# Expert gates scattered into device memory instead of spread by one-hot products

## The chip, the cores and the metric

One core of a Trainium2 chip runs the whole program. TensorE (PE) multiplies, VectorE (DVE) and ScalarE (ACT) work element by element, GpSimd (POOL) does small arithmetic and issues some DMAs, SyncE (SP) issues the DMAs that stream the weights. The metric is the device time of one execution in microseconds (us): the median of three runs of the kernel before is 2316.43 us (2314.47 to 2318.4).

## The reference, cut to what matters

The program is one transformer block (attention and pooling side by side, then a convolutional feed-forward part) and then two layers, each an attention part and a mixture of 16384 single-neuron experts ("peer"), for 256 tokens of width 1024 in float32. The change is in the expert part:

```
q = (x @ w_q).reshape(t, 8, 2, 128)                  # 8 heads, two halves
sc = einsum('thpc,hpnc->thpn', q, sub_keys)          # 128 keys in each half
v_half, i_half = top_k(sc, 16)
cand = v_half[:,:,0,:,None] + v_half[:,:,1,None,:]
cand_idx = i_half[:,:,0,:,None] * 128 + i_half[:,:,1,None,:]
top_s, pos = top_k(cand.reshape(t, 8, -1), 16)
expert = take_along_axis(cand_idx, pos)              # 8 x 16 experts per token
g = softmax(top_s)
act = gelu(einsum('thkd,td->thk', u_tab[expert], x))
y = einsum('thk,thkd->td', g * act, v_tab[expert])
```

Two heads may choose the same expert for a token; their gates then add up.

## The kernel before, in words

The kernel computes all 16384 experts for all tokens and multiplies by a gate that is zero wherever an expert was not chosen. Expert (i, j) has i = 0 to 127 on the partitions and j = 0 to 127 in the loops, and A is a resident tile of 128 x 128 x 256 (i, j, token). Each of the two `peer` layers has three stages.

In `route` 16 tiles of `w_q` give the queries and the scores, and `top16` picks 16 of 128 on DVE. What follows from the scores (candidate sums s0, candidate ids s1, second top-16 s2, the lookup of the chosen ids s4, softmax s3, s3e and s5, transposes s6) is put as small pieces into a list, `self.bg`. In `u_phase` the first expert product runs over 128 values of j: `self.st.get()` fetches a weight tile, `ws_part` issues 24 matmuls into a `tmp` tile, `pop_bg(1)` takes one piece from the list, and every second j `gelu` evicts two columns of A. In `peer` itself the second product follows: `split` turns two columns of A into a rounded part `whi` (ACT) and a remainder `wlo` (DVE), and `acc_k` multiplies them with the tiles of `v`.

The weights come through `Stream`: SP loads a tile of 512 KB into one of four `raw` buffers, ACT rounds it into `hi` (line 86), DVE takes the remainder `lo` (line 87; in `route` POOL does so for every second tile), and three such pairs can be ready ahead of the matmuls. Each engine works in program order, so a `lo` waits behind whatever piece was put on DVE before it.

The gates get into A by one-hot products. When the list is empty, `u_phase` takes four tokens per j: `build` (lines 1372 to 1375) makes on DVE one-hot rows for i and j and multiplies the rows for j by the gate in two float16 parts, and `spread` (lines 1382 and 1383) multiplies them on PE, 8 matmuls for four tokens, so that a bank holds the four tokens' gates for all (i, j). Columns of A that are not computed yet receive the gates by ACT (line 1387); those that are get multiplied by DVE (line 1389). 64 such groups per layer cover 256 tokens. The one-hot rows lie in `xo`, the tile that also holds the residual x, so x is written to device memory (`keep`) at the start of `peer` and read back behind `u_phase`.

Around it: `ffn` is the feed-forward part of the first block. While it runs, `side_step` prepares a vector for its end (`mod`, line 657), to which DVE adds a row `sl` that POOL loads at the start of `ffn`. `gx` and `sl` are constant tiles of 128 x 1024 that several stages use in turn.

Of the kernel before, what the change touches and what calls it, by code (L numbers as in the profile page):

```python
# [20 lines left out]
P = 128  # L21
# [23 lines left out]
class Stream:  # L45
# [56 lines left out]
    def get(self, ahead=NPART):  # L102
        while len(self.ready) < ahead and self.next_item < len(self.items):
            self._prepare()
        return self.ready.popleft()

# [125 lines left out]
class Body:  # L232
# [1002 lines left out]
    def route(self, rt, cv, sk, hi, lo):  # L1235
# [31 lines left out]
        slots = self.sl.bitcast(F16).rearrange("p (i t w) -> p i t w", i=4, w=2)  # L1267
        IT, JT, WH, WL = (slots[:, i] for i in range(4))
        self.slots = (IT, JT, WH, WL)
# [7 lines left out]

        for t in range(2):
# [8 lines left out]
            st["si"] = cv.tile([P, 128], I32, name=f"si{t}")  # L1287
            st["iji"] = cv.tile([P, 2, 128], I32, name=f"iji{t}")
            st["ij"] = cv.tile([P, 2, 128], F32, name=f"ij{t}")
# [8 lines left out]
            bg.append(s0)  # L1298
            bg.append(s1)
            for h in range(0, 8, 2):  # L1300
# [4 lines left out]
                bg.append(s2)  # L1305
# [9 lines left out]
            for h in range(8):  # L1315
                bg.append(lambda h=h, st=st: s4(h, st))

# [7 lines left out]
            bg.insert(len(bg) - 6, s3)  # L1325
            bg.insert(len(bg) - 3, s3e)

            def s5(st=st):
# [4 lines left out]
                nc.vector.tensor_scalar(den, den, WSHIFT, None, op0=OP.mult)  # L1333
                nc.vector.tensor_tensor(e, e, den[:, :, None].to_broadcast([P, 8, 16]), op=OP.mult)
                nc.vector.tensor_copy(st["si"], st["sid"].rearrange("p h k -> p (h k)"))
                nc.vector.tensor_single_scalar(st["iji"][:, 0, :], st["si"], 7, op=OP.arith_shift_right)
# [14 lines left out]
            bg.extend([lambda: None] * 2)  # L1351
            bg.append(s6)

    def u_phase(self, rt, A, hi, lo):

# [274 lines left out]
```

## Time and profile before

| what | us |
|---|---|
| median of 3 runs | 2316.43 (2314.47 to 2318.4) |
| the profiled execution, whole | 2315.69 |
| its span, first to last instruction | 2313.9 |
| PE busy | 2198.4 (95%) |
| DVE busy | 1655.4 (72%) |
| ACT busy | 1098.5 (47%) |
| POOL busy | 160.9 (7%) |
| first layer: `route` about 533 to 588, `u_phase` 588 to 989, second product 989 to about 1330 | |
| second layer: `u_phase` from about 1550, second product to the end | |

An engine's busy time counts overlapping instructions once. [...] The granted TensorE clock is 0.984 of full speed over the span.

### The profile page before, as it was taken

What the parts mean: (1) busy time and instruction counts of PE and PEld (TensorE: products, weight loads), DVE (VectorE), ACT (ScalarE), POOL (GpSimd) and SP (SyncE); (2) the same over time, 40 slices, a digit from 0 to 9 for tenths busy, and PEclk for the clock granted to TensorE, in tenths of its full rate; (3) what the DMA queues carried; (4) which work ended last, traced back from release to release, by engine and by line L of the source; (5) the groups of instructions that cost most, each with busy time, mean ns of one, the idle gap of its engine ahead of it and who ended that gap; (6) DMA issues with size and microseconds to landing.
All of it is one profiled execution on the core that took longest, in us unless ns stands there. A gap on an engine that the chain in (4) does not pass through costs nothing.

```text
span 2313.9 us, 37763 instructions
## 1 busy us (share of the span) xinstructions
PE 2198.4 (95%) x14526; PEld 1988.2 (86%) x14526; DVE 1655.4 (72%) x3410; ACT 1098.5 (47%) x1726; POOL 160.9 (7%) x237
## 2 busy tenths in 40 slices
PE   4888998999999999999999988899999999999998
PEld 3668987778999999988888877799999999888886
DVE  6777755868998899555555565689989985555555
ACT  3445544454444444444444444444444444444444
POOL 2520001303000000000000012120000000000000
PEclk9998999999999999999999999999999999999999
DMA  8856554425565444656666653355544565666664
GB/s 276 317 184 192 177 181 139 141 91 169 175 182 167 156 156 156 210 186 195 192 193 195 189 164 94 114 169 183 183 156 156 156 191 182 191 193 195 193 192 136
DMA packets 114069, 408.88 MB, mean 177 GB/s; under 512 B 12784, under 2 KB 14288, under 8 KB 113632
## 3 DMA queue, kind: packets, MB, share of 16 engines
q1 hardware_dynamic: 110064, 392.71, 53.7%
q0 software_dynamic: 3824, 13.76, 1.9%
q8 instruction: 114, 1.87, 0.3%
q14 instruction: 67, 0.55, 0.1%
HBM read 402.75 MB, written 3.15 MB: 175 GB/s over the span
## 4 chain that ended last, share of the span: by engine, by line
PE 85%; DVE 6%; POOL 2%; ACT 2%; issue 2%; DMA 2%; SPq 0%; POOLq 0%; ACTq 0%; DVEq 0%
PE tmp L483 13%; PE tmp L484 13%; PE tmp L485 13%; PE acc L496 11%; PE acc L497 11%; PE acc L499 11%; DVE lo L87 1%; PE acc L1382 1%; PE acc L1383 1%; PE acc L445 1%; PE acc L446 1%; PE acc L444 1%; POOL rp L526 1%; PE acc L483 1%; PE acc L484 1%
## 5 line engine op out<-in xcount | busy, mean ns | idle before, releaser
L87 DVE TENSOR_TENSOR lo<-raw,hi 128x1024 fp32r<-128x1024 f32 (+3 forms) x683 | 829.8, 1216 | 464.9 <-ACT hi L86 464.0
L86 ACT ACTIVATE hi<-raw 128x1024 fp32r<-128x1024 f32 (+2 forms) x702 | 733.9, 1047 | 554.7 <-PE acc L499 387.3
L483 PE MATMUL tmp<-hThi,hi 128*128 128x256 f32 x2456 | 708.1, 288 | 0.0
L484 PE MATMUL tmp<-hTlo,hi 128*128 128x256 f32 x2456 | 694.0, 283 | 0.0
L485 PE MATMUL tmp<-hThi,lo 128*128 128x256 f32 x2456 | 693.7, 282 | 0.0
L484 PEld LDWEIGHTS tmp<-hTlo,hi 128*128 128x128 f32 x2456 | 470.3, 191 | 0.2 <-issue 0.2
L483 PEld LDWEIGHTS tmp<-hThi,hi 128*128 128x128 f32 x2456 | 470.0, 191 | 0.2 <-ACT hi L86 0.2
L485 PEld LDWEIGHTS tmp<-hThi,lo 128*128 128x128 f32 x2456 | 469.8, 191 | 0.0
L496 PE MATMUL acc<-hi,whi 128*128 128x512 f32 x1024 | 398.6, 389 | 2.4 <-ACT whi L1210 2.4
L497 PE MATMUL acc<-lo,whi 128*128 128x512 f32 x1024 | 398.4, 389 | 0.0
L499 PE MATMUL acc<-hi,wlo 128*128 128x512 f32 x1024 | 315.3, 389 | 0.0
L496 PEld LDWEIGHTS acc<-hi,whi 128*128 128x128 f32 x1024 | 192.2, 188 | 42.6 <-ACT whi L1210 2.8
L497 PEld LDWEIGHTS acc<-lo,whi 128*128 128x128 f32 x1024 | 192.3, 188 | 39.9
L499 PEld LDWEIGHTS acc<-hi,wlo 128*128 128x128 f32 x1024 | 192.2, 188 | 39.9
L1398 ACT ACTIVATE A<-tmp 128x512 f32<-128x512 f32 (+31 forms) x106 | 50.2, 473 | 176.7 <-PE tmp L485 176.7
L1387 ACT ACTIVATE A<-acc 128x328 f32<-128x328 f32 (+31 forms) x128 | 44.9, 351 | 127.9 <-PE acc L1383 127.9
L445 PE MATMUL acc<-lo,hThi 128*128 128x512 f32 (+2 forms) x224 | 88.5, 395 | 10.3 <-DVE lo L87 8.5
L444 PE MATMUL acc<-hi,hThi 128*128 128x512 f32 (+2 forms) x224 | 93.7, 418 | 4.1 <-ACT hi L86 2.0
L446 PE MATMUL acc<-hi,hTlo 128*128 128x512 f32 (+2 forms) x224 | 88.1, 393 | 1.4 <-DVE hTlo L331 1.1
L1211 DVE TENSOR_TENSOR wlo<-A,whi 128x512 fp32r<-128x512 f32 x128 | 87.3, 684 | 0.0
L1210 ACT ACTIVATE whi<-A 128x512 fp32r<-128x512 f32 x128 | 78.3, 613 | 0.0
L1403 DVE TENSOR_TENSOR A<-gx,A 128x512 f32<-128x512 f32 (+16 forms) x84 | 41.6, 496 | 45.6 <-ACT gx L1401 45.5
(394 smaller groups left out, 2730.8 us busy)
## 6 DMA issues: line engine op xcount, KB each, us to landing
raw<-in_uT SPq DMA_DIRECT2D x256, 512.0 KB, 3.5
raw<-in_v SPq DMA_DIRECT2D x256, 512.0 KB, 4.3
raw<-in_w_up SPq DMA_DIRECT2D x44, 512.0 KB, 4.0
adaraw<-in_wada SPq DMA_DIRECT2D x32, 512.0 KB, 5.4
raw<-in_w_q SPq DMA_DIRECT2D x32, 512.0 KB, 3.6
raw<-in_w_down SPq DMA_DIRECT2D x22, 512.0 KB, 3.6
raw<-in_w_in SPq DMA_DIRECT2D x20, 512.0 KB, 5.2
raw<-in_hyb_w_in SPq DMA_DIRECT2D x20, 512.0 KB, 3.7
```

Source lines behind the costliest of these rows:

```text
L86: nc.scalar.activation(hi[:, :width], t[:, :width], AF.Copy)
L87: eng.tensor_tensor(lo[:, :width], t[:, :width], hi[:, :width].bitcast(F32), op=OP.subtract)
L444: nc.tensor.matmul(ps[t][:, :w], xh, wh, start=s, stop=False)
L445: nc.tensor.matmul(ps[t][:, :w], xh, wl, start=False, stop=False)
L446: nc.tensor.matmul(ps[t][:, :w], xl, wh, start=False, stop=e)
L483: nc.tensor.matmul(ps[:, sl], wh, hi[:, k, sl], start=k == 0, stop=False)
L484: nc.tensor.matmul(ps[:, sl], wh, lo[:, k, sl], start=False, stop=False)
L485: nc.tensor.matmul(ps[:, sl], wl, hi[:, k, sl], start=False, stop=k == 7)
L496: nc.tensor.matmul(ps[t][n], h, wh, start=first, stop=False)
L497: nc.tensor.matmul(ps[t][n], h, wl, start=False, stop=False)
L499: nc.tensor.matmul(ps[t][n], l, whi[:, n * 512:(n + 1) * 512], start=False, stop=last)
L1211: nc.vector.tensor_tensor(wl, src, wh.bitcast(F32), op=OP.subtract)
```

## The change

The gates no longer pass through one-hot products. Two tables of 16384 x 256 float32 (16.8 MB each, one per layer) lie in device memory. `clear` fills one with zeros by 8 DMAs of 2 MB from a zeroed `gx`, on POOL's queue: the first table at the start of `ffn`, the second at the start of the first layer's `route`. For each head and each half of the tokens the new piece `s6` computes on DVE the cell numbers (expert times 256 plus token) and the gates, adds to each gate the gates of earlier heads that chose the same expert (lines 1360 to 1363: compare, multiply, reduce, add, over 16 x 16h elements for head h), and issues 16 indirect DMAs on POOL, each of which writes one float32 per partition to 128 cells; behind each stands a one-element memset. A head's DMAs wait until those of the head before, of the same tokens, have landed. In the second product `split` first multiplies A by a tile of gates (128 x 512, 256 KB) that POOL has read from the table, four such tiles ahead. `build`, `spread`, the transposes of the old s6, `keep` and the reload of x are gone. The list is put in another order: the first 15 pieces of the first tokens' half, and then two pieces of the second half for one of the first.

```
@@ ffn
         nc.gpsimd.dma_start(cw, a["cw"])
+        self.clear(0)
         grow = self.row(pf, a["attn_norm"][0:1, :], "grow")
@@ peer
-            keep = self.dramp.tile([2, P, D], F32, name=f"keep{layer}")
-            for t in range(2):
-                nc.gpsimd.dma_start(keep[t], self.x[t])
-            self.route(rt, cv, sk, hi, lo)
-            self.u_phase(rt, A, hi, lo)
-            for t in range(2):
-                nc.gpsimd.dma_start(self.x[t], keep[t])
+            if layer == 0:
+                self.clear(1)
+            self.route(layer, cv, sk, hi, lo)
+            self.u_phase(A, hi, lo)
+            gates = self.gates[layer].rearrange("(i j t) o -> i j (t o)", i=P, t=T)
+            ahead = deque()
+
+            def fetch(j):
+                b = j // 2 % GBUF
+                if b < 2:
+                    g = self.gx[:, b * 512:(b + 1) * 512].rearrange("p (j t) -> p j t", j=2)
+                else:
+                    g = rt.tile([P, 2, T], F32, name="gt", tag="gt", bufs=GBUF - 2)
+                i = nc.gpsimd.dma_start(g, gates[:, j:j + 2, :])
+                if j == 0:
+                    self.after(i, self.last[0] + self.last[1])
+                ahead.append(g)
+
+            for j in range(0, 2 * GBUF, 2):
+                fetch(j)
@@ split, in peer
                 src = A[:, j:j + 2, :]
+                nc.vector.tensor_tensor(src, src, ahead.popleft(), op=OP.mult)
+                if j + 2 * GBUF < P:
+                    fetch(j + 2 * GBUF)
                 wh, wl = whi[:, j % 8:j % 8 + 2, :], wlo[:, j % 8:j % 8 + 2, :]
                 nc.scalar.activation(wh, src, AF.Copy)
@@ route
-            def s6(t=t, st=st):
-                ps = self.acc()
-                for i, s in enumerate((st["ij"][:, 0, :], st["ij"][:, 1, :], st["w"].rearrange("p h k -> p (h k)"))):
-                    nc.tensor.transpose(ps[:, i * P:(i + 1) * P], s, self.ident)
...
+            def s6(h, t=t, st=st):
+                n = h * 16
+                sl = slice(n, n + 16)
+                nc.vector.tensor_scalar(index[:, t, sl], st["sid"][:, h, :], float(T), self.tcol[:, t:t + 1], op0=OP.mult, op1=OP.add)
+                if h == 0:
+                    nc.vector.tensor_copy(total[:, t, sl], st["w"][:, h, :])
+                else:
...
+                    eq = cv.tile([P, 16 * 112], F32, name="dup")[:, :16 * n].rearrange("p (k c) -> p k c", k=16)
+                    both = [P, 16, n]
+                    nc.vector.tensor_tensor(eq, ids[:, None, :n].to_broadcast(both), st["sid"][:, h, :, None].to_broadcast(both), op=OP.is_equal)
+                    nc.vector.tensor_tensor(eq, eq, w[:, None, :n].to_broadcast(both), op=OP.mult)
+                    nc.vector.tensor_reduce(out=total[:, t, sl], in_=eq, axis=AX.X, op=OP.add)
+                    nc.vector.tensor_tensor(total[:, t, sl], total[:, t, sl], st["w"][:, h, :], op=OP.add)
+                now = []
+                for k in range(n, n + 16):
+                    i = nc.gpsimd.indirect_dma_start(out=gates, out_offset=bass.IndirectOffsetOnAxis(ap=index[:, t, k:k + 1], axis=0),
+                                                     in_=total[:, t, k:k + 1], in_offset=None)
+                    for p in now + self.last[1 - t]:
+                        self.tc.declare_no_dep(i.ins, p.ins, reason="distinct cells")
+                    self.after(i, self.last[t])
+                    nc.gpsimd.memset(self.gap, 0.0)
+                    now.append(i)
+                self.last[t] = now
+
+            head = [[lambda h=h, st=st: s4(h, st), lambda h=h, s6=s6: s6(h)] for h in range(8)]
+            work[t] = [s0, s1] + s2s + [s3, s3e, head[0][0], s5, head[0][1]], [x for h in head[1:] for x in h]
+        first, rest = zip(*work)
+        bg.extend(first[0] + rest[0][:4])
+        a_, b_ = deque(rest[0][4:]), deque(first[1] + list(rest[1]))
+        while a_ or b_:
+            for _ in range(2):
+                if b_:
+                    bg.append(b_.popleft())
+            if a_:
+                bg.append(a_.popleft())
@@ u_phase: build and spread are gone; per j one weight tile, one piece of the list, every second j
+                nc.scalar.activation(A[:, j - 1:j + 1, :], ps.rearrange("p (j t) -> p j t", t=T), AF.Gelu)
+    def clear(self, layer):
+        nc.vector.memset(self.gx, 0.0)
+        g = self.gates[layer].rearrange("(p a n d) o -> p a n (d o)", p=P, n=4, d=D)
+        for i in range(8):
+            nc.gpsimd.dma_start(g[:, i], self.gx[:, None, :].to_broadcast([P, 4, D]))
```

On DVE, in the middle of the first layer's list, this stands before: lookups of ids (lines 1308 to 1313), one between two remainders of weight tiles.

```order
L87 TENSOR_TENSOR lo<-raw,hi 128x1024
L1308 TENSOR_TENSOR A<-iota_110,A 128x800
L1312 TENSOR_TENSOR A<-A 128x800
L1313 TENSOR_REDUCE A<-A 128x16
L87 TENSOR_TENSOR lo<-raw,hi 128x1024
```

Near the end of the list, for head 6 of the second half and head 7 after it, this stands there now: the lookup (lines 1326 to 1331) and, between two other remainders, the summing of gates of the same expert (lines 1352 to 1363).

```order
L87 TENSOR_TENSOR lo<-raw,hi 128x1024
L1352 TENSOR_SCALAR sl<-A,tcol 128x16
L1360 TENSOR_TENSOR A<-A 128x1536
L1361 TENSOR_TENSOR A<-A 128x1536
L1362 TENSOR_REDUCE sl<-A 128x16
L1363 TENSOR_TENSOR sl<-sl,A 128x16
L87 TENSOR_TENSOR lo<-raw,hi 128x1024
L1326 TENSOR_TENSOR A<-iota_117,A 128x800
L1330 TENSOR_TENSOR A<-A 128x800
L1331 TENSOR_REDUCE A<-A 128x16
```

Between one remainder and the next there now stands a piece of up to 1792 elements per pass, three passes long.

On POOL, after the seven remainders of the first layer's `route`, the kernel before has only the reload of x and a row.

```order
L87 TENSOR_TENSOR lo<-raw,hi 128x1024 x7
L1200 DMA xo<-keep_5012 128x1024 x2
L1202 DMA sl<-in_attn_norm 128x1024
L1505 DMA caus<-in_caus 128x384
```

Now the 256 scattering DMAs stand there, each with its memset (the first two and the last two of 256 pairs are shown, as two pieces), and behind them the reads of the table.

```order
L87 TENSOR_TENSOR lo<-raw,hi 128x1024 x7
L1366 DMA gates_94<-sl 4194304x1
L1371 MEMSET gap 1x1
L1366 DMA gates_94<-sl 4194304x1
L1371 MEMSET gap 1x1
```

```order
L1366 DMA gates_94<-sl 4194304x1
L1371 MEMSET gap 1x1
L1366 DMA gates_94<-sl 4194304x1
L1371 MEMSET gap 1x1
L1211 DMA gx<-gates_94 128x512 x2
L1211 DMA gt<-gates_94 128x512 x2
```

The first read of the table stands behind the last scatter in POOL's order, besides waiting for all of them to land.

At the start of `ffn` the clear stands ahead of three rows on POOL's queue, where before they followed `cw` at once.

```order
L860 DMA cw<-in_cw 128x88
L1413 DMA gates_94<-gx 128x4x1024 x8
L427 DMA grow<-in_attn_norm 128x1024
L648 DMA sl<-in_bada 128x1024
L427 DMA garow<-in_g_post_ffn 128x1024
```

The rows `sl` and `garow`, which `side_step` uses in the middle of `ffn`, are now behind 16.8 MB of the same queue.

## Rows read from the trace of the kernel before

**Rows 1.** The page, part 1: busy time of each engine.

```profile
PE 2198.4 (95%) x14526; PEld 1988.2 (86%) x14526; DVE 1655.4 (72%) x3410; ACT 1098.5 (47%) x1726; POOL 160.9 (7%) x237
```

**Rows 2.** Stretches: length, busy us (instructions) by engine, clock, DMA share, GB/s.

```profile
50.00:100.00 50.00, 42.95 (x183) 33.09 (x182) 39.85 (x58) 22.78 (x39) 29.20 (x50) 0.93 0.90 333
200.00:240.00 40.00, 40.00 (x336) 40.00 (x335) 31.58 (x46) 23.98 (x42) 0.00 (x0) 1.00 0.69 209
560.00:588.00 28.00, 27.91 (x236) 27.72 (x235) 25.32 (x136) 11.99 (x18) 7.65 (x4) 1.00 0.55 157
625.00:709.00 84.00, 84.00 (x703) 84.00 (x702) 74.99 (x178) 43.05 (x49) 0.00 (x0) 1.00 0.61 183
709.00:900.00 191.00, 191.00 (x1805) 188.63 (x1804) 174.38 (x369) 90.01 (x168) 0.00 (x0) 1.00 0.50 156
989.00:1330.00 341.00, 339.81 (x1499) 281.45 (x1500) 192.22 (x190) 166.37 (x190) 0.00 (x0) 1.00 0.61 192
```

**Rows 3.** Chain of waits, 520 to 990 us: the old transposes.

```profile
651.07 0.33 PE acc L1343 x3
```

**Rows 4.** Timeline of DVE: start, duration, line; pieces of the list between remainders.

```profile
589.44 0.49 DVE L1225 MAX8 A<-acc 128x8 f32<-128x128 f32 x2
...
591.82 1.21 DVE L87 TENSOR_TENSOR lo<-raw,hi 128x1024 fp32r<-128x1024 f32 x1
...
596.45 0.99 DVE L1274 TENSOR_TENSOR A<-A 128x128 f32<-128x128 f32 x8
...
597.48 1.22 DVE L87 TENSOR_TENSOR lo<-raw,hi 128x1024 fp32r<-128x1024 f32 x1
598.62 0.23 DVE L1295 TENSOR_SCALAR A<-A 128x128 f32<-128x128 uint32 x1
...
599.92 0.22 DVE L1276 TENSOR_TENSOR A<-A 128x64 uint16<-128x64 f32 x1
...
601.98 0.32 DVE L1225 MAX8 A<-A 128x8 f32<-128x50 f32 x2
...
603.79 1.23 DVE L87 TENSOR_TENSOR lo<-raw,hi 128x1024 fp32r<-128x1024 f32 x1
...
613.76 0.57 DVE L1308 TENSOR_TENSOR A<-iota,A 128x800 uint16<-128x800 f16 x1
...
615.88 1.21 DVE L87 TENSOR_TENSOR lo<-raw,hi 128x1024 fp32r<-128x1024 f32 x1
```

**Rows 5.** Groups by shape, 575 to 712 us: count | busy us, mean ns.

```profile
L1313 DVE TENSOR_REDUCE A<-A 128x16 f32<-128x800 uint16 x16 | 15.8, 986 | 0.6
L1334 DVE TENSOR_TENSOR A<-A 128x128 f32<-128x128 f32 x2 | 0.6, 292 | 0.1
L1331 DVE TENSOR_REDUCE A<-A 128x8 f32<-128x128 f32 x2 | 0.6, 278 | 0.0
L1274 DVE TENSOR_TENSOR A<-A 128x16 f32<-128x16 f32 x6 | 0.7, 173 | 0.0
```

**Rows 6.** Timelines: POOL and DVE in `ffn`, POOL's issues and a remainder.

```profile
0.28 0.10 POOL L1621 MEMSET const-float32-1.0<- 128x1 f32 x1
15.91 2.11 POOL L696 DMA_DIRECT2D wpool<-in_w_pool  x4 [0.29 <-POOL wpool L693]
181.31 0.53 POOL L645 DMA_DIRECT2D sl<-in_bada  x1
266.95 0.69 DVE L657 TENSOR_TENSOR mod<-tmp,sl 128x512 f32<-128x512 f32 x1 [0.24 <-PE tmp L656]
571.38 2.39 POOL L87 TENSOR_TENSOR lo<-raw,hi 128x1024 fp32r<-128x1024 f32 x1 [4.25 <-ACT hi L86]
```

**Rows 7.** DMA issues: count, KB each, median us to landing.

```profile
wpool<-in_w_pool POOLq DMA_DIRECT2D x4, 16.0 KB, 2.4
```

**Rows 8.** DMA queue of POOL, 0 to 8 us and 15 to 22 us: packets, MB, share.

```profile
q0 software_dynamic: 139, 0.10, 11.3%
...
q0 software_dynamic: 179, 0.09, 7.2%
```

More of the change, by code (lines that the diff above doesn't have):

```diff
@@ L105, in get @@
         return self.ready.popleft()
+GBUF = 4
 class Carve:
@@ L1233, in top16, with route @@
             nc.vector.max_index(u[:, 8:16], v[:, 8:16], r)
-    def route(self, rt, cv, sk, hi, lo):
+    def route(self, layer, cv, sk, hi, lo):
         nc = self.nc
@@ L1266, in route @@
                 bg.append(piece)
-        slots = self.sl.bitcast(F16).rearrange("p (i t w) -> p i t w", i=4, w=2)
-        IT, JT, WH, WL = (slots[:, i] for i in range(4))
-        self.slots = (IT, JT, WH, WL)
+        lay = self.sl.rearrange("p (i t k) -> p i t k", i=4, t=2)
+        index, total = lay[:, 0].bitcast(U32), lay[:, 1]
+        gates = self.gates[layer]
+        self.last = [[], []]
         def cands(dst, v0, v1, eng):
@@ L1276, in cands @@
             eng.tensor_tensor(dst[:, :, off:off + 8], v0[:, :, 8:16], v1[:, :, 0:1].to_broadcast([P, 8, 8]), op=OP.add)
+        work = [None, None]
         for t in range(2):
@@ L1313, in s4 @@
                 nc.vector.tensor_reduce(out=st["sid"][:, h, :], in_=eq, axis=AX.X, op=OP.add)
-            for h in range(8):
-                bg.append(lambda h=h, st=st: s4(h, st))
             def s3(st=st):
@@ L1338, in s5 @@
-                nc.vector.tensor_copy(st["ij"], st["iji"])
-            def s6(t=t, st=st):
-                ps = self.acc()
-                for i, s in enumerate((st["ij"][:, 0, :], st["ij"][:, 1, :], st["w"].rearrange("p h k -> p (h k)"))):
-                    nc.tensor.transpose(ps[:, i * P:(i + 1) * P], s, self.ident)
-                sl = slice(t * P, (t + 1) * P)
-                twice = lambda i: ps[:, i * P:(i + 1) * P, None].to_broadcast([P, P, 2])
-                nc.vector.tensor_copy(IT[:, sl], twice(0))
-                nc.vector.tensor_copy(JT[:, sl], twice(1))
-                nc.vector.tensor_copy(WH[:, sl], twice(2))
-                nc.vector.tensor_tensor(WL[:, sl], twice(2), WH[:, sl], op=OP.subtract)
@@ L1406, in u_phase, with after @@
+    def after(self, i, others):
+        for p in others:
+            self.tc.add_manual_dep(i.ins, p.ins.name, mybir.DependencyInfo(mybir.DependencyClass.Sync, mybir.DependencyReason.DATA))
+    def u_phase(self, A, hi, lo):
+        nc = self.nc
         for j in range(P):
@@ L1409, in u_phase @@
                 ps = self.tmp()
-            new = None
-            if not self.bg and state["g"] < NG:
-                new = (state["g"], build(state["g"]))
-                state["g"] += 1
             w = self.st.get()
@@ L1417, in u_phase @@
             if jj == 1:
-                gelu(s, ps)
-            if last is not None:
-                spread(*last, 2 * s + 2 * jj)
-                state["t"] = last[0] * 4 + 4
-            last = new
-        while last is not None:
-            spread(*last, P)
-            g = state["g"]
-            last = (g, build(g)) if g < NG else None
-            state["g"] += 1
+                nc.scalar.activation(A[:, j - 1:j + 1, :], ps.rearrange("p (j t) -> p j t", t=T), AF.Gelu)
+        self.flush_bg()
+    def clear(self, layer):
+        nc = self.nc
+        nc.vector.memset(self.gx, 0.0)
+        g = self.gates[layer].rearrange("(p a n d) o -> p a n (d o)", p=P, n=4, d=D)
+        for i in range(8):
+            nc.gpsimd.dma_start(g[:, i], self.gx[:, None, :].to_broadcast([P, 4, D]))
     def items(self):
@@ L1487, in run @@
         self.gx = c.tile([P, D], F32, name="gx")
+        self.gates = [self.dramp.tile([P * P * T, 1], F32, name=f"gates{i}") for i in range(2)]
+        self.gap = c.tile([1, 1], F32, name="gap")
+        ti = c.tile([P, 2], I32, name="ti")
+        nc.gpsimd.iota(ti, pattern=[[P, 2]], base=0, channel_multiplier=1)
+        self.tcol = c.tile([P, 2], F32, name="tcol")
+        nc.vector.tensor_copy(self.tcol, ti)
         self.sl = c.tile([P, D], F32, name="sl")
```

59 lines of the change are left out of this document (4 added, 55 removed).

## The prediction

> **What bounds the kernel now.** I read the page's busy times first: PE is busy for 95% of the span [rows 1]. Then the table of stretches: in both parts of `u_phase`, 625 to 709 us with the list and 709 to 900 us with the spreads, and in the second product, PE is busy for the whole stretch or 99.7% of it [rows 2]. So a matmul taken from there is time gained, until another engine is late. The next engine is DVE, 75.0 of 84 us with the list running and 174.4 of 191 us with the spreads [rows 2]. POOL does nothing there. Last I read DVE's timeline for what a piece of the list really costs between two remainders [rows 4].
>
> **Removed: the spreads.** With them 1805 matmuls take 191 us, so a group of 24 + 8 takes 3.386 us; without them 703 take 84 us, so 24 take 2.868 us [rows 2]. A spread costs 0.518 us, 128 of them 66.3 us. The old transposes cost 0.33 us, four times, 1.3 us [rows 3]. Their DVE and ACT work goes with them, beside PE. `keep` and the reload of x lie on POOL's idle queue: nothing.
>
> **Added on DVE, the summing of equal experts.** `u_phase` needs a remainder every 2.868 us. The piece behind a remainder starts 1.14 us after it (598.62 less 597.48) [rows 4]. That leaves 1.73 us per j for a piece. From the starts in [rows 4]: a top-16 of scores 2.38 (589.44 to 591.82), s0 1.03, s1 1.52, s2 1.81, s4 2.12 (613.76 to 615.88). The new s6 for head h makes two passes and a reduction over 256h elements. A two-input pass took 0.292 us for 128 elements [rows 5] and 1.22 for 1024 [rows 4], 0.16 + 0.265h; a reduction 0.278 for 128 and 0.986 for 800 [rows 5], 0.14 + 0.27h; with two 16-wide operations of 0.17 [rows 5] and four gaps of 0.04 that is 0.95 + 0.80h, 6.55 us for head 7. Head 0 takes 0.35, softmax about 1.0.
>
> There are 52 pieces. The first 17 (two top-16, the first half to head 2) sum to 26.5 us, 1.56 each: no lag. The other 35 hold, for the first half, 5 lookups and s6 of heads 3 to 7 (10.6 + 24.75), for the second half everything (57.1): 92.5 us, against 35 x 1.73 = 60.6. DVE falls 32 us behind. Three prepared tiles are the cover: two tiles' matmuls, 5.74 us, less a rounding of 1.05 and a remainder of 1.13, are 3.5 us. The stall is 28 us per layer, 56 us in all. When a DVE piece lasts 6.5 us, the next remainder is queued behind it, and PE waits for that. Ends: 40 us if several pieces' lag falls where PE is ahead; 66 if every piece pays 0.1 us more in gaps.
>
> **Moved: the clears.** 16.8 MB start at 181 us on POOL's queue, and `sl`, issued at 181.31 now, stands behind them; DVE reads it at 266.95 [rows 6], with remainders queued behind that addition. The stretch from 200 to 240 moves 209 GB/s; the fullest stretch moves 333 at a share of 0.90, 370 at a full one [rows 2]. The 161 GB/s left take 104 us, three rows 4 us more: `sl` lands near 289, 22 us late, less 3.5 of cover 18 us. Low end zero, if the clear gets 200 GB/s or more; high end from the same stretch's 209 at 0.69, 303 GB/s in all: 94 left, 178 us, 94 us of wait. I take 18. The second clear has 95 us before its first scatter, and at 157 GB/s beside it (560 to 588) [rows 2] needs 79: nothing, at most 10.
>
> **Added on POOL: 256 scatters per layer.** No row shows an indirect DMA. The nearest is a plain one: four in 2.11 us, 0.53 each, and a small memset of 0.10 [rows 6]: at least 0.63 us a pair, 161 us a layer. At most each waits until the last has landed, 2.4 us [rows 7]: 614 us. I take the plain issue twice (128 addresses are read besides 128 rows) and the memset, 1.2 us, nearer the low row. The first scatter follows piece 13, at 588 + 38 = 626; `u_phase` ends at 588 + 367 + 28 = 983. With 10 us for early heads that wait for the head before to land, and 5 for the first reads, 256 x 1.2 ends at 948. Cover 35 us, break-even 1.34 us a pair: cost nothing.
>
> **Added in the second product.** A multiplication of 0.69 us (128 x 512) [rows 6] for two j: DVE goes from 192 to 236 of 341 us, the reads add 49 GB/s to 192 at a share of 0.61 [rows 2], making 0.77. PE stays the bound: nothing; if the cover went, 128 x 0.69 = 88 us. Single memsets of `gx` hide in the 3.5 us.
>
> **Sum.** Against the profiled execution, 2315.69 us (span 2313.9, 1.8 around it, 0.7 below the median): 2315.7 - 66.3 - 1.3 + 56 + 18 = 2322 us.
>
> [...] POOL's remainder took 2.39 us at 571.38 [rows 6] while DVE was busy for 25.3 of 28 us [rows 2]: no sign that one held up the other. [...]
>
> **Rivals.**
> *The scatters outlast `u_phase`* (slower). PE has nothing to do until the first gate tile, and every 0.1 us above 1.34 a pair costs 51 us over both layers. At 1.6 us: 2322 + 2 x 67 = 2456; at 2.4, 2322 + 2 x 272 = 2866. For it: an idle POOL with 358 us for work that no row prices. Against: plain issues of 0.53. If POOL could not issue while DVE runs a two-input pass, it would have 52 of the 139 us from 626 to the list's end near 765 (40 go to remainders, 32 to s6, 15 to lookups), and behind it 1.73 of each 2.868: the other 270 of its 322 us would take 447, to 1212, 229 us late per layer, 2780. [...]
>
> *The packets crowd out the weights* (slower). 32768 small packets a layer. On POOL's queue 179 packets took 7.2% of 16 engines' 7 us, 45 ns each; 139 took 11.3% of 8 us, 104 ns [rows 8]. That is 92 or 213 us per DMA engine, beside weights at about 0.57 of 358 us, 204 (0.55 to 0.61 in such stretches [rows 2]). At 45 ns all fits; at 104 it is 417, 59 us late per layer: 2440. [...]
>
> *The additions are cheaper* (faster). If the two-input passes of s6 ran at the rate of the 16-bit ones (0.57 us for 800 elements [rows 4]), half the time, the 53 head steps that lag would be 14 us shorter: lag 18, stall 14.5 per layer, 2295; with a clear that makes nobody wait, 2277. For it: PE didn't wait in the list before at 89% of DVE [rows 2]. Against: every 32-bit two-input row takes 1.04 ns for each further element.
>
> **How the numbers follow.** Forecast 0.56, scatters outlast 0.26, packets 0.07, cheaper additions 0.11. The forecast's own range is 2295 to 2360 (stall 40 to 66, clear 0 to some 45). For the whole I leave out the worse half of the scatter rival and little else, and on the fast side reach past 2277: 2270 to 2480. No change means within 0.2%, 2311.8 to 2321.1, about what a measurement can tell. Within the forecast I give faster 0.25, same 0.20, slower 0.55, since stall and clear together must fall from 74 to 63 for faster: 0.14, 0.11, 0.31. With the rivals: faster 0.25, same 0.11, slower 0.64.
>
> **What would show it.** Right: 24 matmuls in 2.87 us early and late in `u_phase`; PE idle before L87 remainders of about 28 us between some 660 and 780 us, DVE full there; `mod` near 267 waiting for `sl`; POOL done before the stretch ends, the second product starting without a wait for gates. Wrong: PE idle for a DMA of the table at the start of the second product; weights that land later than before in `u_phase`; no gap on PE in the list.

## The result and the profile after

The changed kernel takes 2605.5 us against 2317.4 (medians of four runs). One of its runs, 2634.7 us, is in the slow state; the ratio of the other three (2599.3 us on the mean) to before is 1.1217, with a 95% interval of 1.1188 to 1.1246: slower by 12%. Forecast was 2322 us, with a range of 2270 to 2480: the sign was right, the size was not, and the time lies outside the range. The profiled execution took 2586.9 us, its span 2585.1.

First the page of the kernel after, the lines that answer to [rows 1]; the second line is the group of the scatters (count | busy us, mean ns | idle before them):

```profile
PE 2219.0 (86%) x13490; PEld 1983.6 (77%) x13490; DVE 1587.0 (61%) x2929; ACT 1063.8 (41%) x1536; POOL 910.8 (35%) x1398
...
L1366 POOL DMA_INDIRECT gates<-sl x512 | 630.3, 1231 | 240.5 <-issue 135.2
```

PE has 1036 matmuls fewer and is yet busy for 20 us more. POOL went from 161 to 911 us.

Where the time went can be read from the first or last matmul of each stage in the traces (starts in us, taken at the leading line of each product's matmuls: L483 and L496 before, L486 and L499 in the others); e1 and f1 are two kernels of the next section.

| | before | after | e1, no scatters | f1, other places |
|---|---|---|---|---|
| layer 1: first matmul of `route` | 536.9 | 545.3 | 545.3 | 548.0 |
| last matmul of `u_phase` | 988.5 | 1172.9 | 999.6 | 1002.6 |
| first matmul of the second product | 990.2 | 1174.6 | 1001.3 | 1089.5 |
| last one | 1337.6 | 1522.0 | 1348.7 | 1438.7 |
| layer 2: first matmul of `route` | 1502.4 | 1685.5 | 1512.0 | 1603.5 |
| last matmul of `u_phase` | 1954.0 | 2147.6 | 1962.1 | 2053.7 |
| first matmul of the second product | 1955.7 | 2220.9 | 1963.8 | 2144.8 |

The two layers lost their time in different ways. In the first, `route` and `u_phase` grew by 176 us together and nobody waited for gates behind them. In the second, they grew by 10 and the second product began 73 us late. The table of stretches of the kernel after, in the columns of [rows 2]:

```profile
200.00:240.00 40.00, 39.24 (x327) 39.04 (x326) 29.35 (x42) 21.50 (x38) 1.62 (x3) 1.00 1.02 418
560.00:590.00 30.00, 30.00 (x256) 30.00 (x255) 26.63 (x145) 12.43 (x19) 9.56 (x4) 1.00 1.02 415
700.00:800.00 100.00, 82.48 (x614) 79.05 (x613) 95.08 (x115) 34.82 (x40) 80.94 (x121) 0.93 0.41 135
820.00:970.00 150.00, 50.68 (x148) 37.36 (x147) 7.35 (x6) 7.80 (x9) 114.63 (x215) 0.51 0.08 22
1180.00:1521.00 341.00, 341.00 (x1506) 282.38 (x1505) 233.92 (x252) 164.64 (x187) 31.70 (x58) 1.00 0.72 237
1950.00:2140.00 190.00, 190.00 (x1586) 190.00 (x1585) 80.86 (x66) 85.73 (x100) 162.50 (x193) 1.00 0.56 184
2150.00:2210.00 60.00, 0.00 (x0) 0.00 (x0) 0.00 (x0) 0.00 (x0) 46.28 (x89) 0.52 0.02 2
```

The first two lines are the clears. Third, DVE is full while PE has only 614 of some 836 matmuls: the stall of the list. Fourth, the surprise: in 150 us PE gets 148 matmuls done (full pace would be 1254), while DVE and ACT are nearly idle, weights hardly move (22 GB/s) and POOL alone works. Sixth, the same stage of layer 2: full pace, with POOL scattering beside it. Last, PE waits and POOL is still scattering. The granted clock is 0.51 in the fourth and 0.52 in the last, where PE does 148 matmuls and none; that does not make the gaps, which are longer than any matmul there (0.58 us at most), as PE's timeline in the fourth stretch shows:

```profile
864.44 0.37 PE L488 MATMUL tmp<-hThi,lo 128*128 128x256 f32 x1 [1.04 <-issue]
866.54 0.37 PE L486 MATMUL tmp<-hThi,hi 128*128 128x256 f32 x1 [1.73 <-issue]
868.67 0.37 PE L487 MATMUL tmp<-hTlo,hi 128*128 128x256 f32 x1 [1.75 <-issue]
870.77 0.37 PE L488 MATMUL tmp<-hThi,lo 128*128 128x256 f32 x1 [1.73 <-issue]
```

These matmuls belong to one weight tile and wait for no semaphore between them; the starts are 2.10 to 2.13 us apart, and in the whole stretch about half of the distances between matmuls lie near 0.70, 1.40 and 2.10 us, where 0.12 is normal (most of the others are 0.1 to 0.4). I call this a slow stretch below. Others lie at 652 to 661, around 685 and at 1790 to 1800 us.

In layer 2 the waits from 2140 to 2230 us (us in total, times, longest) name what the second product waited for:

```profile
PE acc L499 <- ACT whi L1230: 72.8, 1, 72.8
DVE A L1226 <- DMA gx<-gates: 72.0, 1, 72.0
```

POOL was late because DVE drew its scatters out. The timelines of POOL and of DVE, kernel after, from 2000 us:

```profile
2002.37 1.96 POOL L1366 DMA_INDIRECT gates<-sl  x1 [0.21 <-issue]
2004.33 0.09 POOL L1371 MEMSET gap<- 1x1 f32 x1
2004.64 0.97 POOL L1366 DMA_INDIRECT gates<-sl  x1 [0.22 <-issue]
2005.60 0.09 POOL L1371 MEMSET gap<- 1x1 f32 x1
2005.91 1.91 POOL L1366 DMA_INDIRECT gates<-sl  x1 [0.23 <-issue]
```

```profile
2002.27 1.23 DVE L87 TENSOR_TENSOR lo<-raw,hi 128x1024 fp32r<-128x1024 f32 x1 [1.05 <-ACT hi L86]
2005.76 1.22 DVE L87 TENSOR_TENSOR lo<-raw,hi 128x1024 fp32r<-128x1024 f32 x1 [2.26 <-ACT hi L86]
```

A scatter that meets no remainder takes 0.97 us, and with its memset and the issue a pair takes 1.27. One that starts just behind the start of a remainder takes 1.91 to 1.97; the remainder itself takes what it always took (1.22 and 1.23). The ends tell more: the remainder that starts at 2002.27 ends at 2003.50 and the scatter that it met at 2004.33; the one at 2005.76 ends at 2006.98 and its scatter at 2007.82. Both scatters end 0.83 to 0.84 us behind the remainder, so they stand until DVE is done. A scatter that has already begun isn't held up, as this scatter and the remainder behind it show:

```profile
669.08 0.96 POOL L1366 DMA_INDIRECT gates<-sl  x1 [0.22 <-issue]
```

```profile
669.49 1.22 DVE L87 TENSOR_TENSOR lo<-raw,hi 128x1024 fp32r<-128x1024 f32 x1
```

So the hold-up is one-sided.

### The profile page after: what moved, and what is told of

The parts are those of the page before. It is cut to its first block, busy times and chain, and to the rows that moved or that the text cites. A ratio compares the mean times of both kernels' runs of the same rounds, so it can differ in the third digit from the quotient of the medians.

```text
span 2585.1 us, 36453 instructions
## 1 busy us (share of the span) xinstructions
PE 2219.0 (86%) x13490; PEld 1983.6 (77%) x13490; DVE 1587.0 (61%) x2929; ACT 1063.8 (41%) x1536; POOL 910.8 (35%) x1398
## 5 line engine op out<-in xcount | busy, mean ns | idle before, releaser
L488 PE MATMUL tmp<-hThi,lo 128*128 128x256 f32 x2456 | 719.2, 293 | 92.3 <-issue 45.9
L487 PE MATMUL tmp<-hTlo,hi 128*128 128x256 f32 x2456 | 713.7, 291 | 43.7 <-issue 43.5
L486 PE MATMUL tmp<-hThi,hi 128*128 128x256 f32 x2456 | 717.9, 292 | 36.0 <-issue 34.9
L1366 POOL DMA_INDIRECT gates<-sl x512 | 630.3, 1231 | 240.5 <-issue 135.2
L488 PEld LDWEIGHTS tmp<-hThi,lo 128*128 128x128 f32 x2456 | 488.7, 199 | 105.9 <-issue 54.8
L486 PEld LDWEIGHTS tmp<-hThi,hi 128*128 128x128 f32 x2456 | 489.0, 199 | 52.3 <-issue 52.0
L487 PEld LDWEIGHTS tmp<-hTlo,hi 128*128 128x128 f32 x2456 | 488.8, 199 | 45.0 <-issue 44.8
L499 PE MATMUL acc<-hi,whi 128*128 128x512 f32 x1024 | 399.9, 390 | 74.0 <-ACT whi L1230 74.0
L499 PEld LDWEIGHTS acc<-hi,whi 128*128 128x128 f32 x1024 | 193.0, 188 | 114.5 <-ACT whi L1230 74.4
L1404 ACT ACTIVATE A<-tmp 128x512 f32<-128x512 f32 x128 | 76.4, 597 | 362.2 <-PE tmp L488 203.1
L1211 POOL DMA_DIRECT2D gx<-gates x64 | 34.9, 545 | 420.7 <-DVE A L1226 416.5
L305 POOL TENSOR_TENSOR r<-ms,mhalf 128x1 f32<-128x1 f32 x22 | 15.5, 709 | 386.8 <-DVE ms L301 386.8
L1211 POOL DMA_DIRECT2D gt<-gates x64 | 34.7, 542 | 295.4 <-DVE A L1226 295.4
```

What stands on the lines that cost most here:

```text
L486: nc.tensor.matmul(ps[:, sl], wh, hi[:, k, sl], start=k == 0, stop=False)
L487: nc.tensor.matmul(ps[:, sl], wh, lo[:, k, sl], start=False, stop=False)
L488: nc.tensor.matmul(ps[:, sl], wl, hi[:, k, sl], start=False, stop=k == 7)
L499: nc.tensor.matmul(ps[t][n], h, wh, start=first, stop=False)
L1366: i = nc.gpsimd.indirect_dma_start(out=gates, out_offset=bass.IndirectOffsetOnAxis(ap=index[:, t, k:k + 1], axis=0), in_=total[:, t, k:k + ...
```

## The experiments

**Which part costs what: e1 and e2.** e1 leaves the scatters out:

```diff
-                for k in range(n, n + 16):
-                    i = nc.gpsimd.indirect_dma_start(...)
-                    ...
-                    nc.gpsimd.memset(self.gap, 0.0)
```

> Left out: the indirect DMAs that write the gates into the table and the small memset behind each (the multiplication then reads zeros). All else stays: the summing of equal experts, the clears, the gate reads, the multiplication. Theory A (the loss is made by the scatters themselves: POOL outlasts u_phase by some 70 us in the second layer, and TensorE issues one instruction per 0.7 us in stretches where scatters follow each other unhindered, some 200 us in the first): both go, 2300 to 2330 us, no stretch of u_phase under 50 matmuls per 10 us except the DVE-bound list. Theory B (the summing on DVE starts the slow stretches and the low granted clock keeps them up): they stay, over 2400 us. Theory C (the gate reads and the clears crowd out other transfers): over 2400 us too, with the loss where those run.

Measured: 2331.9 us, 1.0062 of before [1.0046, 1.0079], 2 us over the range of theory A. Theory A holds, B and C fall: by the means, the scatters carry 268 of the 282 us. The table of stretches of e1 shows the list's stall alone and full pace behind it:

```profile
640.00:800.00 160.00, 141.07 (x1075) 137.84 (x1074) 146.39 (x253) 61.62 (x71) 0.54 (x1) 0.94 0.44 152
800.00:960.00 160.00, 160.00 (x1336) 160.00 (x1335) 68.61 (x56) 71.52 (x84) 0.00 (x0) 1.00 0.53 183
```

Against 1336 matmuls, 261 are missing in the first line: 31 us.

e2 leaves out only the summing of equal experts:

```diff
-                if h == 0:
-                    nc.vector.tensor_copy(total[:, t, sl], st["w"][:, h, :])
-                else:
+                nc.vector.tensor_copy(total[:, t, sl], st["w"][:, h, :])
+                if False:
```

> Left out: the search for equal experts and the adding of their weights; the scatters write each head's own weight. Theory A (scatters): DVE has less to do, so scatters run less hindered; the slow stretches of TensorE stay or grow, and the time stays at 2450 to 2700 us. Theory B (the summing starts the slow stretches): none is left; only scatters that outlast u_phase remain, 2270 to 2400 us.

Measured: 2538.6 us. The slow stretch now lies in layer 2, from 1800 to 1960 us, and layer 1 has none (last matmul of `u_phase` at 971.7) but waits 119 us for gates. So neither the summing nor the layer decides. Its table of stretches, one line of each layer:

```profile
860.00:940.00 80.00, 80.00 (x669) 80.00 (x668) 33.76 (x28) 36.27 (x42) 67.73 (x81) 1.00 0.57 185
1820.00:1940.00 120.00, 36.77 (x94) 25.82 (x94) 7.17 (x9) 5.19 (x6) 91.99 (x173) 0.50 0.07 18
```

POOL's instructions, two per scatter, tell the two apart: 81 in 80 us beside remainders, 1.0 per us; 173 in 120 us, 1.44, where PE is slow. I read this as a state that feeds itself: with PE slow there are few remainders, so nothing draws the scatters out, and within a head they come at one per 1.27 us. No run tests that by itself.

**Rate: e3, e5, e4, e8.** e3 takes the remainders off DVE in `u_phase`; ScalarE makes a plain copy in their place:

```diff
+            if fn == "act":
+                nc.scalar.activation(lo[:, :width], t[:, :width], AF.Copy)
...
-            it += [w(a["uT"][layer, j]) for j in range(P)]
+            it += [w(a["uT"][layer, j], eng="act") for j in range(P)]
```

> In u_phase the low part of each weight tile is made by ScalarE as a plain copy (1.05 us) instead of by DVE's subtraction of two operands (1.23 us); the subtraction is left out there. DVE is idle in u_phase once the list is done. If a scatter is drawn out by a DVE instruction with two operands from SBUF (1.9 us beside one, 0.97 without, in the trace of the changed kernel), every scatter takes 0.97 us and a pair 1.27: 256 pairs in 325 us, done before u_phase ends. Theory A (unhindered scatters slow TensorE's issue): TensorE is slow in nearly the whole of these 325 us, in both layers; each layer loses 150 us or more, 2600 to 2900 us. Theory D (the slow stretches have another cause, and only the drawn-out scatters cost time): no wait for gates, no slow stretch, 2280 to 2340 us.

> As e3_act_lo (low parts in u_phase copied by ScalarE, subtraction left out there), and without the scatters and their small memsets. If the copy on ScalarE itself costs nothing, TensorE runs at 83 matmuls per 10 us through both u_phases, DVE's list no longer delays the low parts, and the time is 2265 to 2300 us, under the 2332 of e1_no_scatter by the stall of the list. If ScalarE's extra work is what made e3_act_lo slow, it stays over 2500 us.

> Eight small memsets behind each scatter instead of one, so that a pair takes some 1.9 to 2.1 us even when nothing hinders it. Theory A (it is the rate of the scatters that slows TensorE's issue): no stretch with fewer than 20 matmuls per 10 us while scatters run in u_phase, in either layer; but 256 pairs take 500 to 600 us, so the second product waits for gates for 120 to 220 us in each layer, 2560 to 2760 us. Theory E (any scatter slows it, whatever the rate, because the number of small packets is the same): slow stretches of the same total length stay, and the waits come on top, over 2760 us.

> As e3_act_lo, with three small memsets behind each scatter instead of one: 0.97 us and some 0.6, a pair every 1.56 us with nothing to draw it out. Theory A (slow above some rate between one pair per 1.27 us, where TensorE is slow, and one per 1.7 us, where it isn't): either no slow stretch, and the scatters end some 400 us after the first, 40 to 60 us behind u_phase, 2360 to 2430 us; or, if the limit lies beyond, slow for all of the 400 us, over 2650 us. A time between, with a slowness of half the size throughout, would speak for a cost per scatter in place of a limit.

Measured: e3 2739.5, e5 2271.4, e4 2871.2, e8 2453.9 us. Less work on DVE made the kernel slower by 140 us (e3, one run, against the changed kernel's 2599), and without scatters the same edit costs nothing (e5). In e4, DVE as in the changed kernel, and in e8, DVE idle, a pair takes 2.4 and 1.66 us (the time from the first to the last over 256), and no slow stretch is left in either layer; both pay by waiting for gates, 273 us (1002.5 to 1275.1) and 95 us (966.7 to 1061.4) in layer 1. D falls by e3's time, and E by e4's trace, though e4's time alone would lie in E's range. Both came out over their ranges: in e4 a pair takes 2.24 us from start to start within a head, where I had put down 1.9 to 2.1; in e8 it takes 1.51, under the 1.56 put down, and the mean of 1.66 holds the breaks between heads, which I had left out. One line each, e3 and then e8, in the same stretch:

```profile
860.00:940.00 80.00, 25.58 (x71) 18.71 (x71) 0.00 (x0) 6.60 (x7) 61.19 (x117) 0.50 0.08 20
```

```profile
860.00:940.00 80.00, 80.00 (x669) 80.00 (x669) 0.00 (x0) 62.30 (x71) 61.07 (x198) 1.00 0.59 185
```

POOL is busy for the same 61 us in both; three memsets instead of one between scatters, and PE goes from 71 to 669 matmuls. By starts within a head there is a limit between a pair per 1.27 and one per 1.51 us. e3 itself agrees: while the list still keeps DVE busy, from 770 to 830 us, a pair takes 1.58 us (76 instructions in 60 us), and PE does 486 of some 502 matmuls:

```profile
770.00:830.00 60.00, 59.29 (x486) 58.36 (x485) 57.12 (x71) 44.83 (x52) 51.79 (x76) 1.00 0.57 179
```

**What is scattered: e6, e7, e9 to e15.** All are e3 with other writes in the place of the scatters: plain columns (e6), 512-byte rows (e7, e11), 4-byte values to fixed lists (e9, e10, e12, e13), the fixed list copied by DVE into the computed list's place (e14), and the computed cells with the tokens at other places in a row (e15). The core of three edits:

```diff
# e6
+    i = nc.gpsimd.dma_start(gates.rearrange("(a i b) o -> a i (b o)", a=P, i=P)[k][:, t:t + 1], total[:, t, k:k + 1])
# e10 (e9, e12, e13 with other lists; e7, e11 with rows of 128 from gx)
+    out_offset=bass.IndirectOffsetOnAxis(ap=self.fixed[:, t * P + k:t * P + k + 1], axis=0)
# e15: the token's place; ti holds p + 128 t, tp becomes 128 * (p & 1)
...
+    nc.vector.tensor_single_scalar(ti, ti, 1, op=OP.arith_shift_right)
+    nc.vector.tensor_tensor(ti, ti, tp, op=OP.add)
     nc.vector.tensor_copy(self.tcol, ti)
```

> As e3_act_lo, but each scatter is a plain DMA on the same queue: one column of 128 values of 4 bytes to fixed cells 1 KB apart, no list of addresses (the gates land in the wrong cells). Theory F (reading the addresses and making descriptors from them on POOL is what slows TensorE): no slow stretch, 2270 to 2340 us. Theory G (the stream of 128 small packets per DMA, or of their descriptors, does it): TensorE falls under 20 matmuls per 10 us while these DMAs run back to back, and as a plain issue may be shorter than 0.97 us it lasts for 150 to 330 us a layer, 2400 to 2750 us.

> As e3_act_lo, but each indirect DMA writes 128 rows of 512 bytes (zeros) at a fixed list of 128 neighbouring rows instead of 128 values of 4 bytes at computed cells. Theory H (small writes to device memory are the cause): no slow stretch, or a much weaker one, 2280 to 2450 us. Theories F and G (POOL's work on 128 addresses, or the number of packets): slow as in e3_act_lo, with DMA_INDIRECT at 0.97 us, 2600 to 2850 us.

> As e3_act_lo (2740 us, slow; low parts copied by ScalarE), but the indirect DMAs write their 128 values of 4 bytes to a fixed list of cells 256 bytes apart, 32 KB per DMA, instead of to the computed cells (the gates land in wrong cells). Rows of 512 bytes in neighbouring places were not slow (2282), nor plain columns of 4 bytes 1 KB apart (2270). Theory I (4-byte writes that are far apart, in random places of the 16.8 MB, are what slows TensorE): none slow here, 2275 to 2300 us. Theory J (the indirect form with 4-byte elements does it, wherever they land): slow, 2600 to 2850 us.

> As e9_near4, but the fixed list spreads the cells over the whole table (512-byte row number 20077 times a running number, modulo 32768), all distinct. Theory I: slow as e3_act_lo, 2600 to 2850 us. If it isn't slow (2275 to 2300 us), it isn't the distance either, and what is left is the list itself: that it was computed by DVE just before, and that several values may fall into one place.

> As e7_rows (128 rows of 512 bytes, neighbouring, 2282 us), but with the list of e10_far4: the rows are spread over the whole table. If distance alone decides, slow, over 2500 us; if it takes both distance and writes shorter than 512 bytes, not slow, 2275 to 2320 us.

> As e10_far4 (fixed list, 4-byte values, each cell at the start of a 512-byte row of its own; 2332 us, TensorE not slow), but the order of the rows is scrambled (four rounds of shift, exclusive or and an odd factor), so that the 128 cells of one DMA lie as irregularly in the table as the computed ones, instead of on an even lattice. Theory K (irregular places load some part of the memory more than others, so that 128 writes per 1.27 us are too many): TensorE slow as in e3_act_lo, 2500 to 2850 us. Otherwise 2325 to 2340 us.

> As e10_far4 (even lattice of rows), but partition p writes 4p bytes into its row, as a computed cell does (token number times 4), instead of at its start. Theory L (the place inside the row matters): slow, 2500 to 2850 us. Otherwise 2325 to 2340 us. If neither this nor e12_rand4 is slow, what is left is that the addresses were computed by DVE shortly before.

> As e13_far4_offset (fixed list of spread cells; 2341 us, TensorE not slow), but DVE copies each head's 16 columns of the list, as numbers, into the place of the computed addresses just before that head's scatters. Theory M (what matters is that the addresses are fresh: written by DVE just before POOL reads them): slow as e3_act_lo, 2500 to 2850 us. Theory N (the computed cells themselves matter, where they lie): not slow, 2335 to 2350 us.

> As e3_act_lo (computed cells, 2740 us), but a token's place in its expert's 1 KB row is p/2 + 64t, plus 512 bytes for odd p, so that the 128 cells of one DMA lie in both 512-byte halves of the rows; with the original places all tokens of one DMA lie in the same half, while all fixed lists that weren't slow, the plain columns aside, used both (the gates land at other tokens). Theory O (writing one half alone doubles the load of some part of the memory): not slow, 2330 to 2350 us. Theory N without O, or M: slow, 2500 to 2850 us.

| | written by one DMA | us | matmuls, 860 to 940 us |
|---|---|---|---|
| e3 | 4 B, computed cells | 2739.5 | 71 |
| e6 | plain, 4 B, 1 KB apart | 2270.2 | 669 (DMAs over; 669 too in 660 to 740, beside them) |
| e7 | 512 B, neighbours | 2282.3 | 669 |
| e11 | 512 B, spread | 2279.9 | 669 |
| e9 | 4 B, 256 B apart | 2334.9 | 669 |
| e10 | 4 B, spread evenly | 2332.4 | 669 |
| e12 | 4 B, scrambled | 2342.8 | 669 |
| e13 | 4 B, spread, at 4p in its row | 2340.9 | 669 |
| e14 | as e13, list written afresh | 2339.7 | 669 |
| e15 | 4 B, computed, both halves of the rows | 2338.3 | 669 |

Each of these is one run. Where no slow stretch came, the times of e9, e10, e12 and e13 still lie 1 to 35 us over the ranges put down for that. G falls with e6, F with e7, H and J with e9, I with e10, K, L and M with e12, e13 and e14; O stands. (e7 and e11 are 50 to 60 us ahead of the other lists not because rows are cheaper: their data are ready before the list, so their DMAs start at 595 instead of some 630 us and end within 7 us of `u_phase` in layer 1 and before it in layer 2. The 4-byte lists, at 1.42 us a pair on the mean, end some 30 us behind it in each layer.) e15 against e3 is the sharp pair, since only a token's place in its row differs. Its line of the table of stretches:

```profile
860.00:940.00 80.00, 80.00 (x669) 80.00 (x668) 0.00 (x0) 62.48 (x70) 63.07 (x122) 1.00 0.63 183
```

POOL issues at the rate of e3 (1.27 us within a head in both), and PE is at full pace. With the tokens of one DMA over both 512-byte halves of the experts' rows, no slow stretch is left. No indirect DMA with a fixed list in one half alone was run, so whether the half suffices, or it takes the computed rows as well, isn't shown.

**In the changed kernel: f1.** The places of e15, with the gates read back in that order:

```diff
-                nc.vector.tensor_tensor(src, src, ahead.popleft(), op=OP.mult)
+                halves = lambda v, o: v.rearrange(o, a=2)
+                by_two = halves(src, "p j (b a) -> p j b a")
+                nc.vector.tensor_tensor(by_two, by_two, halves(ahead.popleft(), "p j (a b) -> p j b a"), op=OP.mult)
```

> Complete computation: the changed kernel (2605 us) with one edit, the places of e15_both_halves in the table, and the gates read back in that order by the multiplication. If the half-row places cause the slow stretches in the changed kernel too, none is left in either layer (over 50 matmuls per 10 us from the list's end to u_phase's end), u_phase ends near 1000 us in the first layer as in e1_no_scatter, and what remains of the loss is the wait for scatters drawn out by DVE: 256 pairs at 1.7 to 1.85 us from 638 end at 1075 to 1110, 75 to 110 us of wait per layer, 2480 to 2555 us in all. If slow stretches stay, 2580 us or more.

Measured: 2510.8 us, 1.0834 of before [1.0816, 1.0853]. Three stretches of it:

```profile
640.00:800.00 160.00, 140.93 (x1075) 137.70 (x1073) 148.12 (x257) 61.15 (x70) 125.94 (x187) 0.94 0.49 149
800.00:1000.00 200.00, 200.00 (x1669) 200.00 (x1668) 85.20 (x70) 90.01 (x104) 170.91 (x203) 1.00 0.60 185
1005.00:1080.00 75.00, 0.00 (x0) 0.00 (x0) 0.00 (x0) 0.00 (x0) 58.92 (x113) 0.52 0.02 3
```

The list's stall as in e1 (1075 matmuls), then full pace, then PE waiting 87 us for POOL; in layer 2, 91 us. So the 282 us divide by the means (2317.2 before, 2331.3 e1, 2510.9 f1, 2599.3 after): 14 without scatters (e1 less before), 180 for scatters that outlast `u_phase` (f1 less e1), 88 for the slow stretches (after less f1). In layer 1 of the changed kernel the slow stretches lengthened `u_phase` until the scatters no longer outlasted it, so the split holds for taking the slow stretches away first. That it is the remainders which draw the scatters out shows in f1 against e15, where ScalarE makes a copy in the remainders' place: the 256 pairs of layer 1 take 442 us in f1 (641.4 to 1083.3) and 365 in e15 (632.5 to 997.8), and a scatter lasts 1.33 and 1.03 us on the mean, which makes the 77 us between them.

**Half of it: h1 and h2.** 256 pairs don't fit into `u_phase`, 128 do. h1 keeps the spreads for 128 tokens and scatters the other 128, with three memsets behind each scatter; its table has rows of 512 bytes, so cells of one DMA lie in both halves of 1 KB. h2 also cuts the summing in two pieces and puts empty pieces between:

```diff
-                    bg.extend([look[h], lambda h=h, scat=scat: scat(h)])
+                    bg.extend([look[h]] + rest * (h > 2) + [lambda h=h, same=same: same(h)]
+                              + rest * (h > 3) + [lambda h=h, scat=scat: scat(h)] + rest * (h // 3))
```

> Complete computation. Only the first 128 tokens go by the table (128 indirect DMAs per layer, three small memsets behind each, so that unhindered pairs take 1.56 us); the other 128 keep their spreads, 32 groups instead of 64. From before: 32 spreads of 0.518 us less per layer, 33 us; half of the clears, 4 us more; half of the summing, 28 us of DVE, which the list can take almost without a stall; 128 pairs at 1.6 to 2.3 us are 205 to 295 us, done before u_phase ends. Theory A: no slow stretch, no wait for gates, 2285 to 2305 us. If the scatters beside the spreads are drawn out to 3 us or more, or TensorE slows, 2320 to 2400 us.

> Complete computation. As h1_half (2329 us), where TensorE stood for some 20 us per layer because DVE's list was behind in 650 to 700 us; here the summing of equal experts is cut in two pieces and empty pieces stand between the long ones, so that DVE catches up. If that stall was all that ate the 33 us of the removed spreads, 2283 to 2300 us; if the evened list only moves the wait (spreads begin later and the last ones run after u_phase), 2310 to 2330 us.

Measured: h1 2328.8 us, 1.0041 of before [1.0027, 1.0055], in its second range, but from neither of the causes put down there: no slow stretch, scatters done by 870 us, but the list stalled after all. h2 2293.0 us, 0.9893 [0.9876, 0.9909], in its first range: 1.1% faster than before, little but clear of the noise. From 625 to 709 us, h1 and then h2 (84 us and 703 matmuls in [rows 2]):

```profile
625.00:709.00 84.00, 72.98 (x552) 71.77 (x552) 81.36 (x177) 29.39 (x36) 62.40 (x169) 0.92 0.47 145
```

```profile
625.00:709.00 84.00, 84.00 (x703) 84.00 (x702) 66.16 (x81) 38.78 (x45) 59.12 (x149) 1.00 0.63 182
```

## Why the prediction was wrong

**The step that failed** is "Added on POOL: 256 scatters per layer", costed at nothing on 1.2 us a pair. An unhindered pair takes 1.27, close to it. What was missing is that this is not the price beside the work of `u_phase`: with a remainder every 2.87 us the pairs of f1 average 442 / 256 = 1.73 us, breaks between heads included, and PE waits 87 and 91 us for them. Even with no remainders on DVE the mean is 365 / 256 = 1.43 (e15). Both are beyond the break-even of 1.34 that the prediction itself worked out, and beyond 1.39, which it is with the 15 us of breaks and reads that were set apart there. A second price stood at nothing without a reason: what the scatters do to PE's issue, the slow stretches, 88 us. [rows 6] gave the duration of a plain issue while DVE did not matter to it, and I built on it where the price under the load around it was wanted.

**The rival that came true**, scatters that outlast `u_phase`, had 0.26 and the right arithmetic: 51 us for each 0.1 us above 1.34 makes 2322 + 199 = 2521 at 1.73; f1, the change without the slow stretches, took 2511. Its version in which POOL can't issue during a two-input pass, 2780, lets the remainders go on behind the end of `u_phase`, where f1 has none (DVE x0 from 1005 to 1080). With them ending at 983, the same sum has 270 - 131 = 139 us of POOL's work left then, and 2322 + 2 x 139 = 2600. Its rate was right: 1.2 us in 1.73 of each 2.868 makes 1.99 us a pair, and behind the list f1 takes 1.97 (203 instructions in 200 us).

**The hold-up by DVE.** I let one row ([rows 6], a remainder of 2.39 us on POOL beside mostly one-input work) stand against it. Where DVE is first, the traces of the changed kernel and f1 show the hold-up: of 362 scatters that start inside a remainder, 0.2 us or more before its end, 351 end 0.82 to 0.86 us behind it, and the 85 that start so inside a one-input reduction take 0.96 to 0.98 us, as if alone. Where the scatter is first they show none: of 119 that start 0.15 to 0.9 us ahead of a remainder, 115 take 0.96 to 0.99 us, and the remainders take 1.21 to 1.23, as always.

**The packets, 0.07.** As priced (DMA engines overfull) this is wrong: in the slow stretch their share is 0.08. The trace doesn't show 128 packets a scatter either, but 32, 16 of 32 bytes and 16 of 4. From 820 to 970 us POOL's queue has (packets, MB, share of 16 engines), with the number of scatters below:

```profile
q0 software_dynamic: 3426, 0.06, 1.7%
gates<-sl POOLq DMA_INDIRECT x108
```

That is 12 ns a packet, or 6 us per DMA engine and layer, where the prediction had 92 or 213. That small writes could slow PE by something else than the DMA engines' time was in none of my cases, and is worth 88 us. The size of the writes alone is not it: e9, e10 and e12 to e14 write 4 bytes too, at 1.42 us a pair on the mean, and PE does 669 matmuls from 860 to 940 us in each.

**The other terms.** The spreads: `u_phase` and `route` of layer 2 take 418.9 us in e5 and 451.6 before, 32.7 less per layer; 33.2 forecast. The stall: e1 less e5, 30.3 and 31.2 us for the two layers (`route` to the last matmul of `u_phase`), 61.5; 56 forecast. The summing for head 7 was put at 6.55 us; its three passes in the list of the kernel after (count | busy us, mean ns) make 6.06, and two short operations the rest:

```profile
L1361 DVE TENSOR_TENSOR A<-A 128x1792 f32<-128x1792 f32 x2 | 4.1, 2026 | 0.1
L1362 DVE TENSOR_REDUCE sl<-A 128x16 f32<-128x1792 f32 x2 | 4.0, 2020 | 0.1
L1360 DVE TENSOR_TENSOR A<-A 128x1792 f32<-128x1792 f32 x2 | 4.0, 2018 | 0.0
```

The first clear was oversized: 18 us, while layer 1 starts only 8.4 us late in the changed kernel, for all causes together. I had taken 370 GB/s as full; the stretch moved 418 [rows 2 against the first line of the stretches above]. The mechanism was right: DVE did wait for `sl`, until 275.8 us, and PE for the remainder behind it (waits from 268 to 290 us, in total, times, longest):

```profile
DVE mod L660 <- DMA sl<-in_bada: 5.5, 1, 5.5
PE tmp L488 <- DVE lo L87: 2.6, 1, 2.6
```

The rest of the 8.4 us stays open. The second cost about 5 us (`route` to the last matmul of `u_phase` in e5, 424.0 in layer 1 and 418.9 in layer 2), within its "nothing, at most 10". The second product cost nothing: 347.4 us from first to last matmul before and after in layer 1, with DMA share 0.72 (forecast 0.77). Had the scatters been free, these terms would have made 2315.7 - 65.4 + 61.5 + 8.4 + 5 = 2325 us; e1's profiled execution took 2328, its median 2332. So the forecast was a good price for everything but its largest addition, and I gave that addition's risk too short a range: the better half of a rival with no row for its price. The slow stretches lay outside every rival; without them f1 would still have been over the range.

## What to carry to other kernels

An idle engine is not free time: price what you put on it beside what its neighbours do then, here an indirect DMA that starts beside two-operand work on DVE, 1.9 instead of 0.97 us. When a long job must fit behind another, move only the part that fits (128 of 256 tokens turned +12% into -1.1%), and spread its heavy pieces evenly. Where many small values are scattered back to back, look at where the cells of one DMA lie: here a layout that puts them into both 512-byte halves of the rows took the slow stretches away at no cost in rate.

## What was not expected of the hardware

- 128 scattered 4-byte values per 1.27 us, all in the same 512-byte half of 1 KB rows picked in no order, slow the issue of PE, with gaps near 0.7 us or a multiple of it (148 matmuls in 150 us); at one DMA per 1.51 us (e8), or with cells in both halves (e15), they don't: 669 matmuls in 80 us in each. Plain columns of 4 bytes at one per 0.57 us, which also keep to one half but lie 1 KB apart in order, don't either (e6, 669 in 80 us beside them).
- A scatter that starts inside a remainder on DVE ends 0.84 us behind it; one that starts ahead of a remainder delays nothing (the remainders take 1.21 to 1.23 us).
- The slow stretches hit PE, not DVE or ACT. At 652 to 661 us DVE's eight additions take what they took before [rows 4], and from 820 to 970 us ACT's roundings take 1053 ns on the mean, against 1054 from 1960 to 2130:

```profile
655.58 0.98 DVE L1295 TENSOR_TENSOR A<-A 128x128 f32<-128x128 f32 x8
```

- Why PE, and why that half, stays open. It isn't the DMA engines (weight packets take 187 ns on the mean from 830 to 970 us and 194 from 1960 to 2130) and not the time in which a 16 KB packet of instructions is moved (queue q8: 1.2 us for the one in the first of these stretches, 1.04 on the mean in the second). All runs here are profiled, so a part of the recording in it can't be excluded.
